# One token-mixing and SwiGLU layer in fp32r: the address of the split weights, 64 bytes further on in two stages

## The chip, the cores and the metric

One core of a Trainium2 chip runs the whole layer in one program. The metric is the device time of an execution in microseconds; lower is better. It is given as the median of several runs.

## The reference

The layer takes x (512 tokens of 2048 channels) and a condition c. It computes six rows of modulation from c, and then

```python
h = x * (1.0 + sc_m) + sh_m
y = mixer_sublayer(h, ...)       # projections, HGRN2, sparse attention, merge, w_out
x = layer_norm(ALPHA * x + (1.0 + gt_m) * y, ln1_g, ln1_b)
h = x * (1.0 + sc_f) + sh_f
y = (silu(h @ w_gate) * (h @ w_up)) @ w_down      # 2048 -> 5632 -> 2048
x = layer_norm(ALPHA * x + (1.0 + gt_f) * y, ln2_g, ln2_b)
```

All of it is float32.

## The kernel before

**Products in three parts.** A float32 operand is split into a rounded high part (type fp32r, made by a copy on ScalarE) and a low part (the difference, made on VectorE). `mm3` (line 239) then issues three matmuls for each product: high by high, high by low, low by high. So every weight block of 128x1024 is loaded from memory into a tile `raw`, ScalarE makes `whi` from it (lines 276 and 351), VectorE makes `wlo` (lines 277 and 363), and TensorE reads both. The names `whi` and `wlo` stand for four tiles each, which are used in turn (NW = 4).

**The stages, in order of time.** First the projections of the mixer, with the scans and the attention between them, then the branches `pa` and `pb`, the output projection w_out, gate/up, and w_down. Every matmul of the projections and of w_out streams 512 columns. In w_out (lines 1320 to 1357) the merged activations `mhi`, `mlo` are loaded into the array and the weights are streamed; the last of its four column blocks, c == 3, goes row block by row block (t = 0 to 3), while LayerNorm (`finish1`, line 1145) starts on the rows that are ready.

**Gate/up and w_down by seven products.** Both are block products in which seven products of quarter size stand for eight (`SEVEN`, line 127). For gate/up there are 44 groups of 128 output columns (22 of gate, 22 of up), and seven steps in each. One step (`gu_product`, line 1383) runs over 8 slices; in each, a 128x128 piece of `whi` or `wlo` is loaded into the array and 256 columns of the activations are streamed past it, three matmuls per slice. The activations lie in `mhi`, `mlo`, or in their block sums `R4` to `R7`. The sums of the weight blocks are made on VectorE (`add_behind`, line 1284) or by adding transfers. `prepare` (line 1299) splits a step's weights three steps ahead. In w_down (`dn_product`, line 1502) it is the other way round: pieces of the factors `fhi`, `flo` (the activations) are loaded into the array, and 512 columns of the weights are streamed. The weights of the last eight steps are kept, two in small tiles (`wkhi`, `wklo`) and six in large ones (`wkeep`), and used at the end (line 1683).

**Where the tiles lie.** Tiles come from pools that are laid out one after the other in a partition of SBUF. From the left: `const`; then the pool named `weights`, which holds five `raw` tiles and the eight tiles of `whi` and `wlo`; then `big`, eight tiles of 8 KB (`hThi`, `hTlo`, `mhi`, `mlo`, `wkeep` and others). From the right: the pool of small tiles (`heap`, later `stay`), then `pass` with the sums `R`, which is released when gate/up's last step has been issued, and in its place the pool `tail` (line 1675), which holds w_down's factors. The lines that the change touches:

```python
wp = ctx.enter_context(tc.tile_pool(name="weights", bufs=NW))
bp = ctx.enter_context(tc.tile_pool(name="big", bufs=8))
...
def pair(self):
    return (wp.tile([P, 1024], FR, name="whi", tag="whi"), wp.tile([P, 1024], FR, name="wlo", tag="wlo"))
```

The pools from the left end at byte 149472, where those from the right begin: the partition is full.

**The order of the work** is written out by hand (`manual_schedule`): each engine gets its instructions in the order in which the code calls them, and waits on semaphores for what they need.

Of the kernel before, what the change touches and what calls it, by code (L numbers as in the profile page):

```python
# [25 lines left out]
FT = mybir.dt.float32  # L26
FR = mybir.dt.float32r
# [4 lines left out]
P = 128  # L32
D = 2048
T = 512
NT = T // P
KD = D // P
# [21 lines left out]
NRAW = 5  # L58
NW = 4
# [81 lines left out]
def layer_kernel(ctx, tc, ws, wa, wada, xt, x, cin, bada, lbl, ghg, gcq, gckv, ln1c, lnrow, ident, lvm, dist, out):  # L141
    nc = tc.nc
    mmul = nc.tensor.matmul

    cp = ctx.enter_context(tc.tile_pool(name="const", bufs=1))
    wp = ctx.enter_context(tc.tile_pool(name="weights", bufs=NW))
    bp = ctx.enter_context(tc.tile_pool(name="big", bufs=8))
    hp = tc.alloc_tile_pool(name="heap", bufs=NHEAP, side="right")
    pp = ctx.enter_context(tc.tile_pool(name="psum", bufs=8, space=bass.MemoryType.PSUM))
    dp = ctx.enter_context(tc.tile_pool(name="dram", bufs=1, space=bass.MemoryType.DRAM))  # L150
# [16 lines left out]
    one_t = cp.tile([P, P], FT, name="one_t")  # L167
    lvm_t = cp.tile([P, 7, 256], U8, name="lvm_t")
    idm_t = cp.tile([P, T], U8, name="idm_t")
    bada_t = cp.tile([P, 96], FT, name="bada_t")  # L170
    ada = cp.tile([P, 96], FT, name="ada")
    ada1 = cp.tile([P, 96], FT, name="ada1")
    lb_t = cp.tile([P, DEPTH, HGH], FT, name="lb_t")
# [3 lines left out]
    ln1c_t = cp.tile([P, 2, KD], FT, name="ln1c_t")  # L177
# [6 lines left out]

    cond = cp.tile([P, D], FT, name="cond", tag="row")
    nc.sync.dma_start(cond[:1], cin)
    nc.scalar.dma_start(bada_t, bada)
    nc.gpsimd.memset(one_t, 1.0)
    nc.gpsimd.memset(eps6, 1e-6)
    nc.gpsimd.memset(eps5, 1e-5)  # L190
# [39 lines left out]
    side = Side()  # L230
# [13 lines left out]

    def ada_dot(raw, j, n, parts):

        init = bada_t[:, j:j + 1] if n == 0 else ada[:, j:j + 1]
        w = D // parts
        nc.vector.tensor_tensor_reduce(raw, raw, cond[:, n * w:n * w + w], scale=1.0, scalar=init,
                                       op0=OP.mult, op1=OP.add, accum_out=ada[:, j:j + 1])  # L250

    keys = first_keys()
# [26 lines left out]
    class Stream:  # L279
# [86 lines left out]
                self.load_to(0)  # L366

        def pair(self):
            return (wp.tile([P, 1024], FR, name="whi", tag="whi"), wp.tile([P, 1024], FR, name="wlo", tag="wlo"))

        def get(self, *key, ahead=2):

# [73 lines left out]
    for k in range(KD):  # L446
# [14 lines left out]
        whi, wlo = W.ready.pop(("A", k))  # L461
# [20 lines left out]
        if k in (1, 2):  # L482

            for t in (2 * k - 2, 2 * k - 1):
                ps = bank("early")
                for kk in range(2):
                    hi, lo = hh(kk)
                    s, w = slice(t * P, t * P + P), slice(kk * T, kk * T + T)
# [182 lines left out]
    t = heap("ki")  # L671
# [3 lines left out]
    for p in range(4):  # L675
        whi, wlo = W.get("iq", p)
        for n in range(2):
            ps = bank("qidx")
            for k in range(4):
                w = slice(n * T + k * P, n * T + k * P + P)  # L680
# [179 lines left out]
    for t in range(NT):  # L860
        s = slice(t * P, t * P + P)
        for n in range(2):
            ps = bank("uv")
            w = slice(n * T, n * T + T)
# [3 lines left out]
            ps = ps.rearrange("p (h v) -> p h v", v=SAV)  # L868
# [193 lines left out]
    for n, blk in enumerate((2, 5)):  # L1062
        cols = slice(blk * 16, blk * 16 + 16)
        nc.vector.tensor_scalar_add(ada1[:, cols], ada[:, cols], 1.0)
        ps = bank("grow")
# [8 lines left out]
        return r  # L1074

    gtm = gate_row(0, "gtm")
    colA = cp.tile([P, KD], FT, name="colA")
    colB = cp.tile([P, KD], FT, name="colB")
    nc.vector.tensor_scalar_add(ada1[:, 64:80], ada[:, 64:80], 1.0)
    nc.vector.tensor_mul(colA, ln1c_t[:, 0], ada1[:, 64:80])  # L1080
    nc.vector.tensor_mul(colB, ln1c_t[:, 1], ada1[:, 64:80])
    nc.vector.tensor_add(colB, colB, ada[:, 48:64])


# [148 lines left out]
    def out_mm(ps, t, i, w, first, last):  # L1233
        for kk in range(2):
            hi, lo = mh(2 * i + kk)
            s = slice(t * P, t * P + P)
            mm3(ps, hi[:, s], lo[:, s], *piece(w, kk), first and kk == 0, last and kk == 1)
# [82 lines left out]
    for c in range(4):  # L1320
        if c < 3:
            xs = passing("x")
            for t in range(NT):
                xin_load(xs[:, t], t, c)
            banks = [bank(f"y{t}") for t in range(NT)]
            for i in range(8):
                w = W.get("out", c, i)
                more(1)
                for t in range(NT):
                    out_mm(banks[t], t, i, w, i == 0, i == 7)  # L1330
        else:
            wl = {i: W.get("out", c, i, ahead=min(2, 7 - i)) for i in range(4)}
        for t in range(NT):
            if c == 3:
                ps = bank("y3")
                z = zt[t] = passing("z")
                for n in range(3):
                    nc.gpsimd.dma_start(z[:, n], d_z[t, n])
                z = z[:, 3]
                xin_load(z, t, c)  # L1340
                order = [4, 5, 6, 7, 0, 1, 2, 3] if t == NT - 1 else range(8)
                if t == NT - 1:
                    fetch_behind(-1)
                for n, i in enumerate(order):
                    if i not in wl:
                        wl[i] = W.get("out", c, i, ahead=min(2, 7 - i))
                    out_mm(ps, t, i, wl[i], n == 0, n == 7)
                    if t == NT - 1 and n in (3, 4, 5):
                        del wl[n + 1]
                        prepare(n - 3)  # L1350
            else:
                ps, z = banks[t], xs[:, t]
            nc.vector.scalar_tensor_tensor(z, z, ALPHA, ps, op0=OP.mult, op1=OP.add)
            nc.vector.bn_stats(st1[t][:, c * 6:c * 6 + 6], z)
            nc.gpsimd.dma_start(d_z[t, c], z)
            if c == 3:
                side.add(t, finish1(t))
    side.add(NT - 1, block_sums())
    del banks, xs, wl, w, ps, z, gtm
    W.scale.clear()  # L1360

    def factor(i, k):
# [279 lines left out]
    for step in range(len(steps)):  # L1642
        u = steps[step]
        if step + 3 < len(steps):
            prepare(step + 3)
        fetch_behind(step)
        for ahead, do in ((4, factor_tiles), (8, factor_load)):
            if step + ahead < len(steps):
                v = steps[step + ahead]
                if v.group[0] == "dn" and v.group[2] == 0:  # L1650
                    do(v.i, v.group[1])
        last = step >= len(steps) - KEEP
        if u.group[0] == "gu":
            gu_product(u)
            gu_use(u)
        elif not last:
            dn_product(u)
            dn_use(u)
        add_behind(step)
        if not last:  # L1660
            u.pair = None
        if step == 4 * NPRE + 2:
            for t in range(NT):
                side.drain(t)
            assert not hraw
        if u.group[0] == "gu" and u.group[1] >= NPRE and u.i in ("q7", "q5"):

            nc.gpsimd.tensor_copy(pace, acc_copy[0])
            more(1)
        if step == nsteps - 1:  # L1670
            del m_hi, m_lo
            mh = None
            sums.clear()
            xp.release()
            yp = ctx.enter_context(tc.tile_pool(name="tail", bufs=24, side="right", reuse_waits="tile"))
            small = lambda name, dt=FT: yp.tile([P, T], dt, name=name, tag="y")
            for i in "EYVR":
                part[i] = big(i, FT)
            side.add(0, base_side())
            side.add(1, end_side())  # L1680
# [3 lines left out]
    for t in range(2):  # L1684
# [14 lines left out]
        z = ys[0]  # L1699
# [117 lines left out]
```

## Time and profile before

| | |
|---|---|
| median of 3 runs | 2781.99 us (2778.76 to 2782.38) |
| the profiled execution | 2779.29 us, its span 2777.5 us |
| mean granted TensorE clock | 0.998 |
| TensorE busy | 2749.9 us, 99% of the span |
| VectorE, ScalarE, GpSimd busy | 74%, 42%, 24% |
| chain that ended last | TensorE 92% |
| w_out, c = 0 to 2 | 1277.43 us on, 130.57 us |
| gate/up | from 1456.74 us to about 2347 us |
| w_down | from there to 2765.7 us |

The profile names an instruction by its line, engine and operation, with the tiles that it writes and reads. PE is TensorE's matmul, PEld its weight load, DVE VectorE, ACT ScalarE. A matmul's duration runs from its start until its last result is out, and the next starts long before that; how fast the engine goes is read from the distance of the starts, or from a stretch of time in which it is busy throughout, divided by the number of matmuls in it.

### The profile page before, as it was taken

How to read it: one execution, taken by the hardware profiler on the slowest of the kernel's cores; microseconds unless marked ns; L12 is line 12 of the kernel's file. 1: busy time of each engine (PE TensorE's matmuls, PEld its weight loads, DVE VectorE, ACT ScalarE, POOL GpSimd, SP SyncE). 2: the span in 40 equal slices, each digit the busy share in tenths (PEclk: the TensorE clock that was granted, in tenths of full speed). 3: DMA queues.
4: the chain of work that ended last, by engine and by line, in shares of the span. 5: the costliest groups of instructions: out<-in, count | busy, mean ns of one | idle time of the engine just before them, and what ended most of it. 6: DMA issues, size and time to landing. Idle time of an engine off the chain costs nothing.

```text
span 2777.5 us, 41873 instructions
## 1 busy us (share of the span) xinstructions
PE 2749.9 (99%) x16090; PEld 2439.6 (88%) x16090; DVE 2050.1 (74%) x2904; ACT 1163.5 (42%) x1736; POOL 670.8 (24%) x911
## 2 busy tenths in 40 slices
PE   8999999999999999999999999999999999999998
PEld 6888888888888888788889999999999999888886
DVE  7887787778862688545668877777777777885688
ACT  4334434332222556222246444444444444554453
POOL 0011133333010575421210212221221222750000
PEclk9999999999999999999999999999999999999999
DMA  9867555555984896997945546666555768987775
GB/s 380 302 232 219 158 165 168 179 180 187 319 288 145 229 284 209 271 285 198 293 152 185 191 167 186 185 172 189 171 196 160 192 175 228 323 304 239 244 251 184
DMA packets 179275, 609.87 MB, mean 220 GB/s; under 512 B 23201, under 2 KB 23505, under 8 KB 176001
## 3 DMA queue, kind: packets, MB, share of 16 engines
q1 hardware_dynamic: 126866, 430.18, 45.2%
q0 software_dynamic: 51776, 176.44, 23.8%
q8 instruction: 126, 2.06, 0.3%
q14 instruction: 75, 0.61, 0.1%
q10 hardware_dynamic: 432, 0.57, 0.1%
HBM read 564.09 MB, written 149.70 MB: 257 GB/s over the span
## 4 chain that ended last, share of the span: by engine, by line
PE 92%; DVE 2%; issue 2%; DMA 2%; POOL 1%; ACT 0%; SPq 0%; POOLq 0%; DVEq 0%; ACTq 0%
PE gb L233 6%; PE ga L233 6%; PE V L241 6%; PE V L242 6%; PE V L243 6%; PE y L233 5%; PE pb L233 3%; PE Y L243 3%; PE Y L242 3%; PE Y L241 3%; PE g L233 3%; PE dnV L242 3%; PE dnV L243 3%; PE dnV L241 3%; PE v L233 3%; PE early L233 3%
## 5 line engine op out<-in xcount | busy, mean ns | idle before, releaser
L277 DVE TENSOR_TENSOR wlo<-raw,whi 128x1024 fp32r<-128x1024 f32 x374 | 472.0, 1269 | 253.7 <-ACT whi L276 251.8
L276 ACT ACTIVATE whi<-raw 128x1024 fp32r<-128x1024 f32 x374 | 395.5, 1058 | 315.9 <-PE dnV L243 106.6
L363 DVE TENSOR_TENSOR wlo<-raw,whi 128x1024 fp32r<-128x1024 f32 (+1 forms) x228 | 284.7, 1252 | 107.7 <-ACT whi L351 107.1
L351 ACT ACTIVATE whi<-raw 128x1024 fp32r<-128x1024 f32 (+1 forms) x228 | 234.0, 1039 | 196.9 <-DVE raw L1090 80.2
L242 PE MATMUL V<-mlo,whi 128*128 128x256 f32 x1024 | 290.1, 283 | 0.0
L243 PE MATMUL V<-mhi,wlo 128*128 128x256 f32 x1024 | 290.1, 283 | 0.0
L241 PE MATMUL V<-mhi,whi 128*128 128x256 f32 x1024 | 290.1, 283 | 0.0
L243 PE MATMUL Y<-R,wlo 128*128 128x256 f32 x704 | 199.4, 283 | 0.0
L242 PE MATMUL Y<-R,whi 128*128 128x256 f32 x704 | 199.4, 283 | 0.0
L241 PE MATMUL Y<-R,whi 128*128 128x256 f32 x704 | 199.4, 283 | 0.0
L241 PEld LDWEIGHTS V<-mhi,whi 128*128 128x128 f32 x1024 | 193.2, 189 | 0.0
L242 PEld LDWEIGHTS V<-mlo,whi 128*128 128x128 f32 x1024 | 193.2, 189 | 0.0
L243 PEld LDWEIGHTS V<-mhi,wlo 128*128 128x128 f32 x1024 | 193.2, 189 | 0.0
L241 PE MATMUL dnV<-whi,fhi 128*128 128x512 f32 x352 | 137.0, 389 | 0.0
L243 PE MATMUL dnV<-whi,flo 128*128 128x512 f32 x352 | 137.0, 389 | 0.0
L242 PE MATMUL dnV<-wlo,fhi 128*128 128x512 f32 x352 | 137.0, 389 | 0.0
L241 PEld LDWEIGHTS Y<-R,whi 128*128 128x128 f32 x704 | 132.8, 189 | 0.0
L243 PEld LDWEIGHTS Y<-R,wlo 128*128 128x128 f32 x704 | 132.8, 189 | 0.0
L242 PEld LDWEIGHTS Y<-R,whi 128*128 128x128 f32 x704 | 132.8, 189 | 0.0
L276 ACT ACTIVATE whi<-wrow 128x1024 fp32r<-128x1024 f32 x80 | 84.4, 1055 | 75.8 <-DVE wrow L1288 75.8
L1001 POOL DMA_DIRECT2D sum_dn<-in_ws x132 | 97.6, 829 | 58.2 <-DMA sum_dn<-in_ws 49.9
L233 PE MATMUL ga<-hThi,whi 128*128 128x512 f32 x256 | 101.8, 398 | 0.0
(473 smaller groups left out, 7786.3 us busy)
## 6 DMA issues: line engine op xcount, KB each, us to landing
raw<-in_ws SPq DMA_DIRECT2D x414, 512.0 KB, 5.2
sum_dn<-in_ws POOLq DMA_DIRECT2D x132, 512.0 KB, 8.6
raw<-in_wada SPq DMA_DIRECT2D x128, 512.0 KB, 5.0
raw<-sum_dn SPq DMA_DIRECT2D x88, 512.0 KB, 4.0
rawb<-in_wada SPq DMA_DIRECT2D x22, 1024.0 KB, 11.9
sum_dn<-sum_dn POOLq DMA_DIRECT2D x44, 512.0 KB, 5.1
wrow<-in_ws SPq DMA_DIRECT2D x40, 512.0 KB, 6.6
sum_gu<-in_ws POOLq DMA_DIRECT2D x24, 512.0 KB, 9.2
```

The costliest lines, as they stand in the source:

```text
L233: mmul(*a, **k)
L241: f(ps, ahi, bhi, start=first, stop=False, **k)
L242: f(ps, ahi, blo, start=False, stop=False, **k)
L243: f(ps, alo, bhi, start=False, stop=last, **k)
L276: nc.scalar.activation(hi, src, AF.Copy)
L277: engine.tensor_sub(lo, src, hi.bitcast(FT))
L351: nc.scalar.activation(hi, src, AF.Copy)
L363: nc.vector.tensor_sub(lo, src, hi.bitcast(FT))
L1001: nc.gpsimd.dma_start(d_sum[g, dst], block(g, src), **({"accum_op": OP.add} if add else {}))
```

## The change

The pool `weights` is split. The five `raw` tiles keep a pool of their own (`raw`) ahead of `big`; `whi` and `wlo` get a pool behind `big`. In the last row block of w_out, when the last streamed weights have been used (n == 3), this pool is released, a pool `shift` of one tile of 16 floats is put in its place, and a pool `weights2` of the same eight tiles behind that: from there on, in gate/up and w_down, `whi` and `wlo` lie 64 bytes further on. When `pass` is released, a pool `shift2` of 64 bytes comes ahead of `tail` from the right, so that w_down's factors lie 64 bytes lower. Room for it comes from three small tiles: the bias of the modulation is loaded straight into the accumulator `ada`, and `colA` and `colB` are made in the place of `ln1c_t`.

The addresses that the built programs give, as the remainder by 128 of the tile's first byte in a partition (all pieces that a matmul reads start a multiple of 512 bytes further on):

| matmuls (fp32r) | streamed operand | loaded operand |
|---|---|---|
| all 5888 with 512, 384, 256 or 128 columns up to and with w_out, before and after | 96 | 96 |
| the 96 of the index scores, before and after | 96 | 96 |
| 7392 of gate/up, 256 columns, before | 96 | 96 |
| 7392 of gate/up, after | 96 | 32 |
| 1848 of w_down, 512 columns, before | 96 | 96 |
| 1728 of w_down, after | 32 | 32 |
| 72 of w_down with `wkeep`, after | 96 | 32 |
| 48 of w_down with factors that are made in the pool `stay`, after | 32 | 96 |

The constant `id_t` (streamed in transposes) and `one_t` have 0 in both.

Every engine has the same instructions in the same order in both programs. What differs beside the addresses is which earlier instruction some of them wait for: the first splits of gate/up's weights wait for a later matmul of w_out than before, since the new tiles overlap two old ones each, and two neighbouring loads of the stored rows (`base`, line 1546) have exchanged a wait.

```diff
--- before.py
+++ after.py
@@ -143,8 +143,9 @@
     mmul = nc.tensor.matmul
 
     cp = ctx.enter_context(tc.tile_pool(name="const", bufs=1))
-    wp = ctx.enter_context(tc.tile_pool(name="weights", bufs=NW))
+    wp = ctx.enter_context(tc.tile_pool(name="raw", bufs=NRAW))
     bp = ctx.enter_context(tc.tile_pool(name="big", bufs=8))
+    wq = [tc.alloc_tile_pool(name="weights", bufs=NW)]
     hp = tc.alloc_tile_pool(name="heap", bufs=NHEAP, side="right")
     pp = ctx.enter_context(tc.tile_pool(name="psum", bufs=8, space=bass.MemoryType.PSUM))
     dp = ctx.enter_context(tc.tile_pool(name="dram", bufs=1, space=bass.MemoryType.DRAM))
@@ -167,7 +168,6 @@
     one_t = cp.tile([P, P], FT, name="one_t")
     lvm_t = cp.tile([P, 7, 256], U8, name="lvm_t")
     idm_t = cp.tile([P, T], U8, name="idm_t")
-    bada_t = cp.tile([P, 96], FT, name="bada_t")
     ada = cp.tile([P, 96], FT, name="ada")
     ada1 = cp.tile([P, 96], FT, name="ada1")
     lb_t = cp.tile([P, DEPTH, HGH], FT, name="lb_t")
@@ -184,7 +184,7 @@
 
     cond = cp.tile([P, D], FT, name="cond", tag="row")
     nc.sync.dma_start(cond[:1], cin)
-    nc.scalar.dma_start(bada_t, bada)
+    nc.scalar.dma_start(ada, bada)
     nc.gpsimd.memset(one_t, 1.0)
     nc.gpsimd.memset(eps6, 1e-6)
     nc.gpsimd.memset(eps5, 1e-5)
@@ -244,9 +244,8 @@
 
     def ada_dot(raw, j, n, parts):
 
-        init = bada_t[:, j:j + 1] if n == 0 else ada[:, j:j + 1]
         w = D // parts
-        nc.vector.tensor_tensor_reduce(raw, raw, cond[:, n * w:n * w + w], scale=1.0, scalar=init,
+        nc.vector.tensor_tensor_reduce(raw, raw, cond[:, n * w:n * w + w], scale=1.0, scalar=ada[:, j:j + 1],
                                        op0=OP.mult, op1=OP.add, accum_out=ada[:, j:j + 1])
 
     keys = first_keys()
@@ -366,7 +365,7 @@
                 self.load_to(0)
 
         def pair(self):
-            return (wp.tile([P, 1024], FR, name="whi", tag="whi"), wp.tile([P, 1024], FR, name="wlo", tag="wlo"))
+            return tuple(wq[0].tile([P, 1024], FR, name=n, tag=n) for n in ("whi", "wlo"))
 
         def get(self, *key, ahead=2):
 
@@ -1074,11 +1073,10 @@
         return r
 
     gtm = gate_row(0, "gtm")
-    colA = cp.tile([P, KD], FT, name="colA")
-    colB = cp.tile([P, KD], FT, name="colB")
+    colA, colB = ln1c_t[:, 0], ln1c_t[:, 1]
     nc.vector.tensor_scalar_add(ada1[:, 64:80], ada[:, 64:80], 1.0)
-    nc.vector.tensor_mul(colA, ln1c_t[:, 0], ada1[:, 64:80])
-    nc.vector.tensor_mul(colB, ln1c_t[:, 1], ada1[:, 64:80])
+    nc.vector.tensor_mul(colA, colA, ada1[:, 64:80])
+    nc.vector.tensor_mul(colB, colB, ada1[:, 64:80])
     nc.vector.tensor_add(colB, colB, ada[:, 48:64])
 
 
@@ -1345,8 +1343,16 @@
                     if i not in wl:
                         wl[i] = W.get("out", c, i, ahead=min(2, 7 - i))
                     out_mm(ps, t, i, wl[i], n == 0, n == 7)
+                    if t == NT - 1 and n == 3:
+                        for k in range(4, 8):
+                            del wl[k]
+
+                        del w
+                        wq[0].release()
+                        shift = ctx.enter_context(tc.tile_pool(name="shift", bufs=1))
+                        shift.tile([P, 16], FT, name="shift")
+                        wq[0] = ctx.enter_context(tc.tile_pool(name="weights2", bufs=NW, reuse_waits="tile"))
                     if t == NT - 1 and n in (3, 4, 5):
-                        del wl[n + 1]
                         prepare(n - 3)
             else:
                 ps, z = banks[t], xs[:, t]
@@ -1356,7 +1362,7 @@
             if c == 3:
                 side.add(t, finish1(t))
     side.add(NT - 1, block_sums())
-    del banks, xs, wl, w, ps, z, gtm
+    del banks, xs, wl, ps, z, gtm
     W.scale.clear()
 
     def factor(i, k):
@@ -1672,6 +1678,9 @@
             mh = None
             sums.clear()
             xp.release()
+
+            shift2 = ctx.enter_context(tc.tile_pool(name="shift2", bufs=1, side="right"))
+            shift2.tile([P, 16], FT, name="shift2")
             yp = ctx.enter_context(tc.tile_pool(name="tail", bufs=24, side="right", reuse_waits="tile"))
             small = lambda name, dt=FT: yp.tile([P, T], dt, name=name, tag="y")
             for i in "EYVR":
```

## Rows read from the trace of the kernel before

**Rows 1.** The page, part 1: busy us (share of the span) xinstructions.

```profile
PE 2749.9 (99%) x16090; PEld 2439.6 (88%) x16090; DVE 2050.1 (74%) x2904; ACT 1163.5 (42%) x1736; POOL 670.8 (24%) x911
```

**Rows 2.** Stretches: us, busy by engine (xinstructions), clock, DMA share, GB/s; gate/up, w_down.

```profile
core 0: us, PE busy (x) PEld busy (x) DVE busy (x) ACT busy (x) POOL busy (x), PEclk, DMA share, GB/s
1540.30:2346.90 806.60, 806.60 (x6724) 806.60 (x6723) 621.94 (x703) 368.98 (x503) 168.40 (x300) 1.00 0.62 181
2346.90:2765.70 418.80, 418.80 (x1850) 346.84 (x1849) 328.35 (x351) 207.63 (x251) 102.08 (x81) 1.00 0.78 265
```

**Rows 3.** The chain that ended last, in w_out: start us, us, what.

```profile
1277.43 130.57 PE y L233 x576
```

**Rows 4.** Lines by form, TensorE: count | busy us, mean ns of one.

```profile
L241 PE MATMUL V<-mhi,whi 128*128 128x256 f32 x1024 | 290.1, 283 | 0.0
...
L241 PE MATMUL dnV<-whi,fhi 128*128 128x512 f32 x352 | 137.0, 389 | 0.0
...
L241 PEld LDWEIGHTS V<-mhi,whi 128*128 128x128 f32 x1024 | 193.2, 189 | 0.0
```

**Rows 5.** Timeline in gate/up, matmuls and loads: start us, us, engine, line, operation.

```profile
1599.92 0.28 PE L243 MATMUL V<-mhi,wlo 128*128 128x256 f32 x1
1600.04 0.29 PE L241 MATMUL V<-mhi,whi 128*128 128x256 f32 x1
...
1599.93 0.19 PEld L241 LDWEIGHTS V<-mhi,whi 128*128 128x128 f32 x1
1600.05 0.19 PEld L242 LDWEIGHTS V<-mlo,whi 128*128 128x128 f32 x1
```

**Rows 6.** Lines 198 and 1166: timeline, then durations min/median/max of matmul and load.

```profile
14.79 1.39 PE L198 MATMUL cond<-one_t 128*128 128x128 f32 x11
L198 PE MATMUL cond<-one_t x29: 275/275/276, 14.8 to 17.9; 128*128 128x128 f32 x29
L198 PEld LDWEIGHTS cond<-one_t x56: 192/192/334, 9.5 to 18.0; 128*128 128x128 f32 x56
1435.94 1.03 PE L1166 MATMUL zt<-id_t,z 128*128 128x128 f32 x8
...
L1166 PE MATMUL zt<-id_t,z x64: 270/272/328, 1423.2 to 1467.1; 128*128 128x128 f32 x64
L1166 PEld LDWEIGHTS zt<-id_t,z x64: 138/140/143, 1423.0 to 1467.0; 128*128 128x128 f32 x64
```

**Rows 7.** Timeline of score matmuls with 512 columns.

```profile
930.13 0.40 PE L233 MATMUL s<-rlo,qb 128*128 128x512 f32 x1
930.36 0.62 PE L233 MATMUL s<-rhi,qb 128*128 128x512 f32 x2
930.82 0.39 PE L233 MATMUL s<-rlo,qb 128*128 128x512 f32 x1
931.05 0.39 PE L233 MATMUL s<-rhi,qb 128*128 128x512 f32 x1
931.28 0.39 PE L233 MATMUL qb<-rhi,whi 128*128 128x512 f32 x1
```

**Rows 8.** Timelines where w_out ends and gate/up begins.

```profile
1450.18 0.39 PE L233 MATMUL y<-whi,mlo 128*128 128x512 f32 x1
...
1452.00 2.04 ACT L276 ACTIVATE whi<-raw 128x1024 fp32r<-128x1024 f32 x2
...
1453.25 2.35 DVE L277 TENSOR_TENSOR wlo<-raw,whi 128x1024 fp32r<-128x1024 f32 x2
...
1456.74 0.28 PE L241 MATMUL V<-mhi,whi 128*128 128x256 f32 x1
```

**Rows 9.** Gate/up on VectorE: its longest wait (us, times, longest), then lines by form.

```profile
DVE wlo L277 <- ACT whi L276: 157.8, 129, 1.6
L277 DVE TENSOR_TENSOR wlo<-raw,whi 128x1024 fp32r<-128x1024 f32 x202 | 245.4, 1223 | 159.4 <-ACT whi L276 157.8
...
L1297 DVE TENSOR_TENSOR raw<-raw,wrow 128x1024 f32<-128x1024 f32 x40 | 48.7, 1218 | 0.0
```

## The prediction

> **What bounds the kernel now.** I read the busy shares first [rows 1]. TensorE is busy for 2749.9 of 2777.5 us and no other engine is over 75%, so only a change in what TensorE itself does, or a wait put in front of it, can move the end. The profiled execution took 2779.29 us around that span, 2.7 us below the median of 2781.99 us; I make the sum in differences and put it on the median.
>
> Then the table of stretches [rows 2]. [...] With 6724 matmuls there, one starts every 806.60 / 6724 = 120.0 ns (the few records that the edges cut shift this by less than 0.1 ns). The w_down stretch gives 418.80 / 1850 = 226.4 ns, and the first three column blocks of w_out 130.57 / 576 = 226.7 ns [rows 3]. The reader should note in the lines by form that the durations of single matmuls (283 and 389 ns) and loads (189 ns) are latencies that overlap [rows 4]; the pace is what sums to the span.
>
> The pace splits in two. [...] So 256 columns are worth 106.7 ns, and 13.3 ns remain on every matmul, at 256 and at 512 columns alike. In gate/up there are 44 groups of 7 products, each of 8 slices of three matmuls, 7392 in all: the remainder is 7392 x 13.3 ns = 98.6 us there. Next to each matmul a weight load for the next one begins some 10 ns after the matmul does [rows 5], so a load and a streamed operand are under way at the same time. By place I mean what is left of a tile's byte address when it is divided by 128. Before the change both operands of every one of these matmuls have the place 96. The change makes that 32 against 96 for gate/up, and for nothing else that is large.
>
> **The change, part by part.**
>
> *Order of the work.* No engine gets an instruction more or less or in another order. So every cost must come from an address, or from a wait that an address moves.
>
> *Gate/up's weights 64 bytes further on: 7392 matmuls with 256 columns.* The trace has no such matmul with operands at two places, so I bound it. Gain, largest: the whole remainder goes, 98.6 us. Gain, by a row: the transposes (line 1166) are the only matmuls in quantity whose operands have different places, 0 and 96; eight of them take (1.03 - 0.27) / 7 = 108.6 ns apiece [rows 6]; at that pace gate/up would lose 7392 x 11.4 = 84 us. They are another operation, with a shorter load (140 ns against 189), so this is an end and no forecast. Between: the full fp32 matmuls of line 198 have both operands at place 0, a similar load (the median is 192 ns), and take (1.39 - 0.275) / 10 = 111.5 ns [rows 6]. So a load of this size does not in itself force 120 ns; at 111.5 the gain would be 62.8 us. Loss: the nearest row is the score matmuls of qb at 512 columns, which go at 1.15 / 5 = 230 ns from 930.13 to 931.28 us [rows 7], 3.3 ns over the 226.7 of the same form elsewhere; 7392 x 3.3 = +24 us. Nothing excludes a loss altogether.
>
> I take half of the remainder: 120.0 to 113.3 ns, 7392 x 6.67 ns = **49 us** less. My reason: a load reads 512 bytes of a partition while the matmul reads 1024, so the faster stream overruns a lead of 64 bytes soon, and I expect the two to be kept apart in only part of each load. 113.3 is close to the 111.5 of line 198, the row with the nearest load, and on the careful side of it.
>
> [...]
>
> *w_down's factors 64 bytes down.* There the weights stream and the factors are loaded. Both move by 64 bytes modulo 128, so 1728 of 1848 matmuls keep equal places (32 and 32). The other 120 get places 64 bytes apart: 72 with the kept weights of the last steps, 48 with the factors made before the new pool exists. Even the whole remainder on them is 120 x 13.3 = 1.6 us either way. I put 0.
>
> *The new pool's waits.* Its first tiles lie over two old ones each, so the splits of the first three gate/up weights must now wait for the last matmul that reads the old weights. That one starts at 1450.18 us; ScalarE makes the first whi at 1452.00 and VectorE the first wlo at 1453.25 [rows 8]. What holds them is ScalarE's work on the transposes before, and the raw weights are there. Cost 0; if that cover were gone, the slack to the first gate/up matmul at 1456.74 would still be over 2 us.
>
> *Smaller edits.* The bias of the adaLN rows is read into the accumulator, and the two LayerNorm columns are scaled in place: same instructions, same sizes, 0. In the tail pool two neighbouring loads of stored rows exchange a wait and are issued in the same order, 0.
>
> *What is late next.* With 113.3 ns the gate/up stretch of 806.6 us shrinks to 761.6. VectorE's 621.94 us [rows 2] go from 77% to 82% of it, ScalarE's from 46% to 48%. VectorE's longest waits there are for ScalarE's whi, 157.8 us in 129 pieces, none over 1.6 us [rows 9]; they are the room in that chain, and by the code weights are split three steps (3 x 24 x 113.3 ns = 8.2 us) ahead. DMA has a share of 0.62. I put 0 for a new bound.
>
> Sum: 2781.99 - 49 = **2733 us** (2730 against the profiled execution's own 2779.29).
>
> **Rivals.** *No effect.* The remainder is a fixed cost of changing weights and has nothing to do with places. For it: it is the same 13.3 ns at 256 and 512 columns, in every stage, whichever buffer the tiles lie in, as a fixed cost would be; a clash of two streams should feel their length. [...] Against it: line 198 changes weights as often and shows 111.5 [rows 6]. Time: 2782, give or take 5.6 us, the 0.2% that a measurement of this kernel can tell from no change.
>
> *Slower.* The equal place is the good one. If the offset makes the streamed operand overtake the load, the load may be held up instead of the matmul, and with 256 columns it has no spare time: one begins with each matmul, and the next 120 ns on. With 512 columns it has twice that, which is why such a clash could hide in the rest of the kernel. It decides once the pace passes 120.8 ns (0.75 ns x 7392 = 5.6 us). Priced by the 3.3 ns of the qb rows: 2782 + 24 = 2806. For it: a load shows 189 ns beside a pace of 120 [rows 4], so it is the longer of the two. Against it: line 198 shows loads going in every 111.5 ns.
>
> *Part of the gain is lost.* TensorE would go at 113.3, but the splits come late at the denser places of each group of seven steps, where four block sums of 1.22 us and seven splits of 1.22 us [rows 9] stand on VectorE. If a third is given back: 2782 - 33 = 2749. For it: VectorE is at 77% already. Against it: the waits there are VectorE's, not TensorE's.
>
> **Numbers.** Forecast 0.50, part lost 0.12, no effect 0.20, slower 0.18; so faster 0.62, same 0.20, slower 0.18. The range runs from 2698, the 84 us of the transposes' pace, up to 2790, which takes in no effect and the mildest losses; most of the slower case is left out above, and the loss of the whole remainder below.
>
> **What would show it.** The gate/up stretch at 1.00 clock should hold 6724 matmuls in about 762 us, while the w_out stretch keeps 226.7 ns and w_down about 226.4. If gate/up stays at 120.0, the fixed cost was right. If it is over 120.8 and the loads show more than 189 ns, the slower rival. If single starts are 113 apart but gaps with VectorE as releaser stand between the steps, part was lost. A change of w_down's pace, or of any stage before 1456 us, would mean that something other than the relative place matters, and my reading is wrong at its root.

## The result, and the profile after

The changed kernel takes 2747.48 us (median of 20 executions), the kernel before 2780.6 us beside it. The ratio is that of the means, 2758.63 and 2780.72 us: 0.9921, 95% interval 0.9895 to 0.9946. It is faster, by 22 us where 49 were forecast. The median hides the shape: 12 of the 20 executions lie between 2744 and 2749 us and 8 between 2772 and 2781, none between. I call these the lower and the upper group; the median falls in the lower one, and so is 33 us under the one before. The profiled execution (2745.55 us, span 2743.8, mean granted clock 0.998) is of the lower one.

The page of the changed kernel, part 1, answers to [rows 1]:

```profile
PE 2716.5 (99%) x16090; PEld 2391.9 (87%) x16090; DVE 2044.0 (74%) x2904; ACT 1158.0 (42%) x1736; POOL 688.3 (25%) x911
```

As many instructions as before, on every engine, and TensorE still fills the span. So the time went in TensorE's pace. Stretches of the changed kernel, with the columns of [rows 2]; the first two lie in gate/up, the third in w_down:

```profile
core 0: us, PE busy (x) PEld busy (x) DVE busy (x) ACT busy (x) POOL busy (x), PEclk, DMA share, GB/s
1580.00:1980.00 400.00, 400.00 (x3532) 400.00 (x3531) 326.52 (x369) 189.41 (x263) 100.12 (x160) 1.00 0.63 191
2000.00:2280.00 280.00, 280.00 (x2473) 280.00 (x2473) 228.21 (x260) 132.42 (x185) 73.68 (x115) 1.00 0.65 191
...
2400.00:2700.00 300.00, 300.00 (x1287) 241.38 (x1286) 218.92 (x245) 146.82 (x172) 27.49 (x21) 1.00 0.76 250
```

Gate/up: 400.00 / 3532 = 113.25 ns, and 113.3 from start to start (the matmuls cut by the edges make such quotients 0.1 to 0.3 ns too small). That is the forecast to the digit. But w_down goes at 300.00 / 1287 = 233.1 ns, 233.3 from start to start, where it went at 226.7. That was not forecast. The lines by form say the same in latencies, against 283 and 389 ns in [rows 4]:

```profile
L241 PE MATMUL V<-mhi,whi 128*128 128x256 f32 x1024 | 282.7, 276 | 0.0
...
L241 PE MATMUL dnV<-whi,fhi 128*128 128x512 f32 x352 | 138.9, 395 | 0.0
```

The account by stage, from the starts of the first and the last matmul of each:

| stage | before, us | after, us | difference |
|---|---|---|---|
| up to gate/up | 1456.7 | 1458.0 | +1.2 |
| gate/up | 890.2 | 843.4 | -46.8 |
| w_down | 418.7 | 430.4 | +11.8 |
| the end behind it | 11.8 | 11.8 | 0.0 |
| span | 2777.5 | 2743.8 | -33.7 |

Gate/up starts between 1456.0 and 1459.7 us in the profiles below, with the same work ahead of it, so the first row is scatter. The third is some 1700 matmuls times 6.67 ns (11.4 us), and a little from those that have other addresses.

One more thing stands in the early part of gate/up. This is the timeline of TensorE in the changed kernel around one short stall:

```profile
1497.76 0.28 PE L242 MATMUL Y<-R,whi 128*128 128x256 f32 x1
1497.87 0.28 PE L243 MATMUL Y<-R,wlo 128*128 128x256 f32 x1
1497.99 0.28 PE L241 MATMUL Y<-R,whi 128*128 128x256 f32 x1
1498.11 0.28 PE L242 MATMUL Y<-R,whi 128*128 128x256 f32 x1
1498.82 0.38 PE L243 MATMUL Y<-R,wlo 128*128 128x256 f32 x1 [0.43 <-DVE wlo L276]
...
1500.08 0.28 PE L241 MATMUL Y<-R,whi 128*128 128x256 f32 x1
1500.19 0.28 PE L242 MATMUL Y<-R,whi 128*128 128x256 f32 x1
1500.31 0.28 PE L243 MATMUL Y<-R,wlo 128*128 128x256 f32 x1
1500.42 0.28 PE L241 MATMUL Y<-R,whi 128*128 128x256 f32 x1
```

Ahead of the stall 117.8 ns from start to start, behind it 113.3. The same operands at the same addresses have two paces here, and TensorE changed from one to the other where it had stood still. After the last such stall (1564 us) the remaining 6503 matmuls keep 113.3. What TensorE waited for between 1455 and 2300 us (the waits view; the first row is the transposes, line 1166 in [rows 6], the last of which stand between gate/up's first steps; the row of PEld is the stall at 1564 us, where the matmul itself stood for 0.1 us):

```profile
PE zt L1164 <- DVE z L1153: 1.2, 2, 0.8
PE Y L243 <- DVE wlo L276: 0.4, 1, 0.4
PE A L243 <- DVE wlo L276: 0.2, 1, 0.2
...
PEld V L241 <- ACT e L1418: 0.3, 1, 0.3
```

### The profile page after: what moved, and what is told of

Same layout as the page of the kernel before. It is cut to its first block, busy times and chain, and to the rows that moved or that the text cites. A ratio compares the mean times of both kernels' runs of the same rounds, so it can differ in the third digit from the quotient of the medians.

```text
span 2743.8 us, 41871 instructions
## 1 busy us (share of the span) xinstructions
PE 2716.5 (99%) x16090; PEld 2391.9 (87%) x16090; DVE 2044.0 (74%) x2904; ACT 1158.0 (42%) x1736; POOL 688.3 (25%) x911
## 4 chain that ended last, share of the span: by engine, by line
PE 90%; DVE 3%; DMA 2%; issue 2%; ACT 2%; POOL 1%; SPq 0%; DVEq 0%; ACTq 0%; POOLq 0%
PE gb L233 6%; PE y L233 6%; PE ga L233 6%; PE V L241 5%; PE V L243 5%; PE V L242 5%; PE early L233 3%; PE g L233 3%; PE dnV L241 3%; PE dnV L243 3%; PE dnV L242 3%; PE v L233 3%; PE pb L233 3%; PE Y L243 3%; PE Y L241 3%; PE Y L242 3%
## 5 line engine op out<-in xcount | busy, mean ns | idle before, releaser
L243 PE MATMUL V<-mhi,wlo 128*128 128x256 f32 x1024 | 282.8, 276 | 0.0
L241 PE MATMUL V<-mhi,whi 128*128 128x256 f32 x1024 | 282.7, 276 | 0.0
L242 PE MATMUL V<-mlo,whi 128*128 128x256 f32 x1024 | 282.7, 276 | 0.0
L241 PE MATMUL Y<-R,whi 128*128 128x256 f32 x704 | 194.4, 276 | 0.0
L242 PE MATMUL Y<-R,whi 128*128 128x256 f32 x704 | 194.4, 276 | 0.0
L248 DVE CUSTOM_DVE_ANT_0 raw<-raw,cond,ada 128x1024 f32<-128x1024 f32 x128 | 166.5, 1314 | 1.1 <-DMA raw<-in_wada 0.8
```

The source lines that it names most:

```text
L241: f(ps, ahi, bhi, start=first, stop=False, **k)
L242: f(ps, ahi, blo, start=False, stop=False, **k)
L243: f(ps, alo, bhi, start=False, stop=last, **k)
```

## The experiments

Two theories stand against my prediction's account. **By 256:** what counts is the difference D between the byte address of the loaded operand and that of the streamed one, modulo 256. Before the change D is 0 in gate/up and w_down. After it gate/up has D = 64, and w_down 128 (factors at 160, weights at 32), which modulo 128 looks like 0. **Two paces:** where a D has two paces, the start after a stall settles which, and the two groups of times are executions that end up in the one or the other. The rival to the first is that w_down suffers from something else in the new pools; to the second, that the upper group is a matter of clock, chip or another stage.

All edits are to the changed kernel. Its two shift tiles have 16 floats (64 bytes) each.

**w_down equal modulo 256.**

```diff
-            shift2.tile([P, 16], FT, name="shift2")
+            shift2.tile([P, 48], FT, name="shift2")
```

> The changed kernel with 192 bytes instead of 64 ahead of w_down's factors, so that streamed weights and loaded factors have the same address modulo 256 (32 and 32) and not only modulo 128 (32 and 160 in the changed kernel). Theory A, what counts is the difference of the two addresses modulo 256: w_down goes back from 233.3 to 226.7 ns a matmul, gate/up stays at 113.3; 1728 x 6.67 ns = 11.5 us less than the changed kernel, 2734 us against its 2745.5. Theory B, what counts is each operand's address modulo 128 (both 32 in either kernel): w_down stays at 233.3 ns, 2745 us. Theory C, w_down's slowing has nothing to do with addresses but follows from gate/up ending sooner: also 233.3 ns.

Median 2733.72 us of 6 (5 between 2732.0 and 2736.1, one at 2764.3), ratio 0.9853, interval 0.9822 to 0.9884. Its stretches in gate/up and w_down:

```profile
1580.00:1980.00 400.00, 400.00 (x3532) 400.00 (x3531) 325.76 (x368) 189.28 (x262) 100.09 (x160) 1.00 0.63 191
...
2400.00:2700.00 300.00, 300.00 (x1326) 248.39 (x1325) 227.73 (x259) 154.27 (x186) 27.94 (x21) 1.00 0.78 258
```

w_down is back at 226.7 ns (300.00 / 1326 = 226.2), gate/up keeps 113.3, and the lower group lies 11 us under that of the changed kernel, which is what w_down's term comes to. The 64 bytes by which the diff moved the factors cost these 11 us; moved by 192 they cost 0.6 (w_down takes 419.3 us here and 418.7 before). Theories B and C, with 233.3 ns, fall. Weights 64 bytes up and factors 192 down are 256 apart in sum, so at 512 columns a period of 256 is shown (226.7 ns at 0 and at 256) and not a longer one; at 256 columns the runs go from 0 to 192 and don't test it. The time is the forecast's number, by a kernel that isn't the one forecast.

**The changed kernel beside itself.**

> The changed kernel itself once more, for its two groups of times (2744 to 2749 us and 2772 to 2781 us). If the groups belong to the chip or to one loading of the program, all runs here fall in one of them; if each execution falls anew, both appear, about one in three in the upper. If its profile is of the upper group: gate/up at 120.0 ns with w_down at 226.7 would mean that both changed paces are gone together (2780); gate/up at 120.0 with w_down at 233.3 would give 2792, above what was seen; gate/up at 113.3 with long waits would mean something off TensorE.

Eleven executions on one chip: 5 between 2744.1 and 2745.4, 6 between 2771.9 and 2775.6. Both groups occur on one chip, from one execution to the next.

**D = 128 and D = 192 in gate/up.**

```diff
-                        shift.tile([P, 16], FT, name="shift")
+                        shift.tile([P, 32], FT, name="shift")
```

with `shift2` as in the changed kernel, so that w_down gets D = 64:

> Gate/up's weights 128 bytes further on instead of 64 (difference 128 modulo 256, equal modulo 128), w_down's factors as in the changed kernel, which gives w_down a difference of 64 modulo 256. Theory A: gate/up at a pace of its own, neither 120.0 nor 113.3 necessarily, and slower than 120.0 if 256 columns behave as 512 did at a difference of 128 (126.7 ns, +49 us); w_down near the 229 to 230 ns that the 120 odd matmuls of the changed kernel showed. Theory B (modulo 128): gate/up at 120.0, as before the change, w_down at about 229.

2781.56 us. And the same line with 48 floats, which gives gate/up D = 192 and w_down D = 0 with both operands at 160:

> Gate/up's weights 192 bytes further on (difference 192 modulo 256; 64 modulo 128, as in the changed kernel), w_down's factors as in the changed kernel, so that w_down has equal addresses modulo 256, both 160. Theory A: w_down at 226.7 ns although both operands moved; gate/up not necessarily at 113.3, since 192 is not 64. Theory B: gate/up at 113.3, and w_down at 233.3, since both operands have 32 modulo 128 as in the changed kernel.

2765.02 us. Gate/up and w_down, first for D = 128 and 64:

```profile
1580.00:1980.00 400.00, 400.00 (x3373) 400.00 (x3373) 311.40 (x351) 182.66 (x251) 85.26 (x150) 1.00 0.62 182
...
2400.00:2700.00 300.00, 300.00 (x1288) 241.70 (x1287) 222.64 (x234) 146.87 (x172) 55.95 (x40) 1.00 0.76 252
```

then for D = 192 and 0:

```profile
1580.00:1980.00 400.00, 400.00 (x3399) 400.00 (x3398) 313.47 (x355) 184.91 (x254) 86.77 (x150) 1.00 0.62 182
...
2400.00:2700.00 300.00, 300.00 (x1325) 248.40 (x1324) 227.76 (x242) 150.80 (x177) 53.69 (x38) 1.00 0.79 258
```

From start to start: 118.7 and 233.3 ns, then 117.8 and 226.7. Equal places are good for the 512 columns of w_down (226.7) wherever both lie (0 by difference: at 224, 32 or 160), and bad for the 256 columns of gate/up (120.0). With D = 192 TensorE never stands still after 1469 us, so that run can't tell a single pace of 117.8 from the upper of two. Theory B falls in both runs: it had 120.0 and 229, then 113.3 and 233.3. Theory A held in the pace of its own at 128 and in w_down's 226.7, but its bracket for w_down at D = 64, 229 to 230, was 3 to 4 ns low.

**Stops in gate/up and w_down.** The four runs that follow make TensorE stand still 26 times, at every 16th step, 17 times in gate/up and 9 in w_down:

```diff
+    for n in range(40, len(steps) - 16, 16):
+        steps[n].stop = True
+
+    def stop(ps, e):
+
+        nc.vector.scalar_tensor_tensor(e, ps[:, :1], 0.0, e.bitcast(FT), op0=OP.mult, op1=OP.add)
...
+            if k == 3 and u.stop:
+                stop(ps, wlo[:, 4 * P:4 * P + 1])
```

(and a like call in w_down's loop). The next matmul needs that column of wlo, VectorE needs the sum as it stands. First with D = 64 and 0, as in the first experiment:

> The kernel with both pools moved (gate/up 64 bytes apart, w_down equal modulo 256) and 26 stops: at every 16th step VectorE reads one column of the running sum and rewrites one column of the second half of wlo with its own value (0 times the sum added), so that TensorE stands still once for some 0.5 to 3 us and starts anew. Theory (which of two locked paces TensorE falls into is settled when it starts after standing still): every one of the 17 stretches of gate/up between stops holds one pace from its first ten matmuls on, 113.3 or 117.8 ns, both appear, and changes happen at stops alone; w_down stays at 226.7 in all its stretches. Rival (113.3 is the pace of this address and 117.8 is a matter of the early part of gate/up, its other instructions or the DMA traffic there): 113.3 in all 17 stretches. Rival (the pace drifts with load or time): changes between stops. The time is some 2734 plus 26 stops of 0.5 to 3 us, 2750 to 2810.

The stops were longer than expected, since VectorE's own work stands ahead of them (in the 6.00 us from 1969 us on, within one stop, VectorE is busy for 4.37): 2.1 to 6.5 us from start to start in gate/up, and behind 15 of the 17 there the granted clock was 0.50 for some 3 to 6 us. So the time, 2882.70 us, is over the range I gave, and says nothing here. The paces do. A stop in the timeline of TensorE:

```profile
1968.79 0.28 PE L243 MATMUL V<-mhi,wlo 128*128 128x256 f32 x1
1974.69 0.58 PE L241 MATMUL V<-mhi,whi 128*128 128x256 f32 x1 [5.63 <-DVE wlo L1395]
1975.07 0.41 PE L242 MATMUL V<-mlo,whi 128*128 128x256 f32 x1
```

and stretches between four successive stops, at a granted clock of 1.00:

```profile
1940.00:1968.00 28.00, 28.00 (x250) 28.00 (x248) 22.39 (x25) 12.25 (x17) 3.17 (x7) 1.00 0.57 194
1985.00:2020.00 35.00, 35.00 (x299) 35.00 (x298) 25.88 (x31) 16.64 (x22) 2.92 (x7) 1.00 0.47 159
2030.00:2065.00 35.00, 35.00 (x312) 35.00 (x311) 28.36 (x32) 16.54 (x23) 7.02 (x14) 1.00 0.49 156
```

112.0, 117.1 and 112.2 ns by the quotients; from start to start 113.3, 117.8 and 113.3. Of the 17 stretches behind stops 14 have 113.3 and 3 have 117.8, each the same to its end once the first ten matmuls at a clock of 1.00 are past (from there on its sixths agree to a few hundredths of a nanosecond), none in between. The clock (1.00 in all three rows), the share of DMA (0.47 at 117.8 ns, 0.49 and 0.57 at 113.3) and the instructions don't go with it. The nine stretches of w_down, at D = 0, all have 226.7.

The same with D = 192 in gate/up:

> The same 26 stops, with the gate/up weights 192 bytes further on instead of 64 (w_down equal modulo 256 again). In the run without stops gate/up stayed at 117.8 ns from first to last and TensorE never stood still. Theory (192 is 64 seen from the other operand and has the same two paces; that run merely started in the slower one and had no stall to leave it): some of the 17 stretches at 113.3. Rival (192 has the one pace 117.8): 117.8 in all 17. Time 2765 plus the stops, 2780 to 2840.

2888.97 us, over the range for the same reason. Three successive stretches of gate/up:

```profile
1640.00:1675.00 35.00, 35.00 (x299) 35.00 (x298) 25.94 (x28) 16.33 (x23) 2.91 (x7) 1.00 0.52 169
1685.00:1720.00 35.00, 35.00 (x312) 35.00 (x310) 27.57 (x33) 16.87 (x23) 7.63 (x13) 1.00 0.56 160
1740.00:1772.00 32.00, 32.00 (x274) 32.00 (x274) 22.43 (x27) 13.90 (x20) 7.44 (x13) 1.00 0.64 160
```

D = 192 has the same two paces, with the other one as the usual one: 2 of 17 at 113.3, 15 at 117.8. The rival of a pace of its own falls.

Then D = 96 in both stages, and D = 32 in both (weights 24 and 8 floats on, factors 16 and 48 down):

> The same 26 stops, gate/up 96 bytes apart modulo 256 and w_down 96 bytes apart too (weights 96 bytes on, tail pool 64 down). Theory (the pace goes by the difference modulo 256, in steps as fine as 32 bytes): gate/up between the paces of 64 and 128, 113.3 to 118.7, and w_down 233.3, the pace of its neighbours 64 and 128. Rival (only the difference in units of 64 bytes counts): 96 gives just the paces of 64, or just those of 128.

> The same 26 stops, gate/up 32 bytes apart modulo 256 and w_down 32 too (weights 32 bytes on, tail pool 192 down). Theory (fine steps): gate/up between the paces of 0 and 64, 113.3 to 120.0, w_down 226.7 to 233.3. Rival (units of 64 bytes): gate/up as at 0, 120.0 in all stretches, and w_down 226.7 in all.

2893.10 and 2896.66 us. Stretches of gate/up and one of w_down, for D = 96 and then for 32:

```profile
1640.00:1675.00 35.00, 35.00 (x297) 35.00 (x296) 26.20 (x31) 16.14 (x22) 3.47 (x8) 1.00 0.47 155
1835.00:1870.00 35.00, 35.00 (x301) 35.00 (x300) 28.71 (x33) 15.80 (x24) 8.48 (x13) 1.00 0.68 182
2435.00:2465.00 30.00, 30.00 (x130) 24.12 (x129) 23.07 (x20) 14.69 (x17) 17.75 (x11) 1.00 0.80 277
...
1690.00:1725.00 35.00, 35.00 (x298) 35.00 (x298) 28.04 (x33) 15.96 (x22) 8.86 (x15) 1.00 0.50 144
2435.00:2470.00 35.00, 35.00 (x152) 28.18 (x151) 26.07 (x24) 16.82 (x19) 20.02 (x16) 1.00 0.85 307
```

From start to start, with 96 gate/up has 117.3 in 6 stretches and 118.7 in 11, w_down 234.3 in all nine; with 32 it is 118.3 in all 17 and 233.3. So 32 bytes matter, and the rival that counts in units of 64 falls. My bracket for 96, between 113.3 and 118.7, held; for w_down I was 1 ns low.

**The upper group.** Twice the changed kernel once more, for a profile of an execution in the upper group:

> The changed kernel once more, to see an execution of the upper of its two groups of times (2772 to 2781 against 2744 to 2749 us). Theory: where the time is in the upper group, gate/up's pace after its last stall (some 1564 us) is 117.8 ns to the end, 4.4 ns x 6503 matmuls = 29 us more, and w_down the same 233.3; where it is in the lower group, 113.3. Rival: the upper group has 113.3 too, and its 27 us are elsewhere (a lower clock, stalls, another stage).

> As the run before it: 117.8 ns in gate/up after the last stall if its time is over 2770 us, 113.3 if it is under 2750.

2744.94 and 2744.74 us: both lower, with 113.3 as in the first profile, so they tell nothing of the upper one.

**The weights' pool alone.**

```diff
-            shift2 = ctx.enter_context(tc.tile_pool(name="shift2", bufs=1, side="right"))
-            shift2.tile([P, 16], FT, name="shift2")
```

> Only the weights' new pool, 64 bytes further on; w_down's factors stay where they were before the change. Then w_down's difference is 192 modulo 256 (the factors' address less the weights'). Theory (difference modulo 256): w_down at the 229.0 to 229.6 ns that 120 matmuls with this difference showed in other runs, 1752 x 2.7 ns = 4.7 us over the kernel with both at the same place, so a lower group at 2738 to 2739 us, an upper one at some 2768. Rival (equal places modulo 128 are good for w_down, 64 apart is bad, as my prediction had it): w_down at up to 233.3 ns, 11.7 us over, 2745 to 2746.

Four executions between 2734.8 and 2737.6 us, one at 2777.8. The changed kernel on the same chip took 2744.9 and 2744.7 us, so half of the change alone is 8.5 us better than the whole, in the lower group: the second half, the factors' move, did only harm. The profile is of the one at 2777.8, with a granted clock of 0.997 like the others:

```profile
1580.00:1980.00 400.00, 400.00 (x3399) 400.00 (x3398) 313.65 (x354) 183.17 (x251) 86.75 (x150) 1.00 0.63 183
...
2400.00:2700.00 300.00, 300.00 (x1288) 242.99 (x1287) 221.34 (x233) 145.49 (x170) 52.56 (x39) 1.00 0.76 251
```

Gate/up is at 117.8 from 1470 us to its end, without a stall, and w_down at 233.3, where I had expected 229.0 to 229.6 for D = 192. The lower group lies under the 2738 to 2739 that I had expected, the upper one over its 2768. No profile of this kernel shows the lower group. But in every kernel with gate/up at D = 64 the first 48 matmuls of w_down have D = 192 (the factors made in the pool `stay`). The second and the 47th of them are shown here, first of the first experiment's profile, then of a profile of the same kernel in the upper group (2764.44 us, see below):

```profile
2303.39 0.39 PE L242 MATMUL dnV<-wlo,fhi 128*128 128x512 f32 x1
2313.69 0.39 PE L242 MATMUL dnV<-wlo,fhi 128*128 128x512 f32 x1
...
2331.58 0.40 PE L242 MATMUL dnV<-wlo,fhi 128*128 128x512 f32 x1
2342.08 0.40 PE L242 MATMUL dnV<-wlo,fhi 128*128 128x512 f32 x1
```

10.30 / 45 = 228.9 ns and 10.50 / 45 = 233.3. So D = 192 has two paces at 512 columns too. With both, 7331 x 4.4 = 32 us in gate/up and 1752 x 4.4 = 8 us in w_down are the distance between this kernel's groups, 41.6 us (an estimate for the lower group, from the 228.9 of the other kernel).

**One stall less.** On the kernel with w_down equal modulo 256, three sums of the first group of seven steps come one step earlier:

```diff
-            adds.setdefault(s - ahead, []).append((("gu", n), what))
+            early = n == NPRE and what in ("S3", "S1", "S2")
+            adds.setdefault(s - ahead - early, []).append((("gu", n), what))
```

> The kernel with w_down equal modulo 256, and for the first group of seven steps three weight sums on VectorE one step earlier, so that the stall at 1563 to 1566 us (0.34 and 0.22 us) goes. Theory (the pace is drawn at each start after a stall, and the last one decides): no stall after 1501 us, the pace holds from there to the end; the lower group at 2733 to 2734 us, and executions in the upper group (2764) are left only where the start at 1500 us falls badly, fewer than the 6 to 7 in 10 lower ones that two draws in a row would give. Rival (what decides is something else, such as the chip or the moment): the same share of upper executions as without the edit, or the stall moves to another place.

Median 2733.38 us, five executions between 2731.8 and 2735.2, ratio 0.9833, interval 0.9819 to 0.9846. The stall at 1563 us is gone. Whether that keeps executions out of the upper group, five can't say, so it ran again beside the kernel without the edit, and the changed kernel with them:

> The kernel with w_down equal modulo 256 again, beside the next one on the same chip: lower group 2732 to 2736, upper some 2764 (1 of 6 so far). If two draws in a row decide, at 19 good in 24 each as the stopped run showed, some 4 in 10 executions are in the upper group; if it is rarer, the draws at these starts are better than those after long stops.

> The three sums early again: median 2733.4 as before, and if the last stall was worth a draw, fewer upper executions than the run beside it; if the share is the same in both, the stall at 1563 us has nothing to do with it.

> The changed kernel again, with more executions, for the share of the upper group (so far 13 of 33) and for a profile of one. Theory: a profile at 2772 us or more shows gate/up at 117.8 ns from its last stall to its end and w_down at 233.3; one under 2750 shows 113.3. Rival: 113.3 in both, the difference elsewhere.

Without the edit 2733.95 us (one of 6 in the upper group, at 2764.4), with it 2734.20 (2 of 6, at 2763.6 and 2764.7), the changed kernel 2759.55 (6 of 12; median between the groups). With the earlier runs it is 2 of 12 and 2 of 11: the edit did nothing that can be seen, and the idea that this stall was a draw worth saving isn't borne out. Nor are the 4 in 10 that two draws at 19 in 24 would give; the stretches counted above make the chance of one draw 14 in 17.

But two of these profiles fell in the upper group. The kernel without the edit, at 2764.44 us, around 1497 us:

```profile
1496.38 0.28 PE L241 MATMUL Y<-R,whi 128*128 128x256 f32 x1
1496.49 0.28 PE L242 MATMUL Y<-R,whi 128*128 128x256 f32 x1
1497.61 0.39 PE L243 MATMUL Y<-R,wlo 128*128 128x256 f32 x1 [0.84 <-DVE wlo L276]
...
1499.48 0.28 PE L243 MATMUL Y<-R,wlo 128*128 128x256 f32 x1
1499.60 0.28 PE L241 MATMUL Y<-R,whi 128*128 128x256 f32 x1
```

and its stretches:

```profile
1500.00:2300.00 800.00, 800.00 (x6794) 800.00 (x6794) 630.06 (x720) 371.12 (x514) 172.42 (x298) 1.00 0.62 184
...
2400.00:2700.00 300.00, 300.00 (x1325) 248.41 (x1324) 229.08 (x243) 151.81 (x177) 51.70 (x38) 1.00 0.79 260
```

113.3 ahead of the stall, 117.8 behind it and for all 7077 matmuls that remain (800.00 / 6794 = 117.75), with w_down at 226.7 and the clock at 1.00. 7077 x 4.4 ns = 31 us is the distance from 2733.7 to 2764.4. The second profile, at 2763.62 us, shows the same. The upper group is the upper pace; a lower clock or another stage has no part in it. At 117.8 the splits keep up and TensorE doesn't stand still any more (busy for all 800.00 us), not even at 1563 us, so that the upper pace, once it has come through 1500 us, stays to the end. That the changed kernel's own upper group is the same is argued from its distance (some 31 us): its five profiles were all of the lower group.

The paces from start to start that the profiles of these runs show, in nanoseconds:

| D, bytes | 256 columns (gate/up) | 512 columns (w_down) |
|---|---|---|
| 0 | 120.0 | 226.7 |
| 32 | 118.3 | 233.3 |
| 64 | 113.3 or 117.8 | 233.3 |
| 96 | 117.3 or 118.7 | 234.3 |
| 128 | 118.7 (120.0 in the first 48) | 233.3 |
| 192 | 113.3 or 117.8 | 228.9 or 233.3 |

The 72 matmuls with `wkeep`, also at D = 192 in the changed kernel, go at 229.5 within their short runs. Of the 1728 in the prediction's count 24 read kept weights that lie in the factors' own pool and have D = 0 in every kernel.

## Why the prediction was wrong, step by step

**Gate/up's pace** was right: 113.3 ns, and 46.8 of the 49 us in the profiled execution. The rest went to four stalls of 0.2 to 0.7 us and to the early part at 117.8. With not an instruction more or less, the pace went from 120.0 to 113.3 ns by where the loaded and the streamed operand lie; that it is their reads that clash fits this, but no run shows the mechanism. That the number came out to the digit is luck: it was half of a remainder. That remainder of 13.3 ns is my estimate too, 120.0 less the 106.7 by which 226.7 is above it; no run shows it as a part of a matmul, and what the runs show in its place is 113.3 to 120.0 ns at 256 columns, by D. And the reason that I gave for half of the remainder, a lead of 64 bytes that is soon overrun, isn't shown by anything. By it a lead of 128 should have done better, and it measured 118.7.

**w_down's factors: this step failed.** I wrote "Both move by 64 bytes modulo 128, so 1728 of 1848 matmuls keep equal places" and put 0. Both moved, but in opposite directions, +64 and -64, and what counts in the runs at 512 columns is the difference modulo 256, which became 128 (233.3 ns, where 0 has 226.7). The term measured +11.8 us, and the first experiment takes all but 0.6 of it away by an edit of one number. Nothing in the trace had told me 128; every matmul of the large stages had D = 0 there, so 128 and 256 fitted equally well, and I should have priced the other one: the 3.3 ns of the qb rows [rows 7] at 512 columns would have been 1728 x 3.3 = 6 us, half of the loss. The prediction named this sign itself: a change of w_down's pace would show its reading wrong at its root.

**Two paces at one address** weren't among the rivals, and so were put at nothing. Before the change D = 0 had shown only one (120.0 ns in gate/up), and the sum takes a single pace for all executions. 8 of 20 lie 31 us higher, which is 12.5 us in the mean. So of the 27 us between the forecast of 49 and the 22 of the means, 2.5 went in gate/up itself, 11.8 in w_down and some 12.5 to the upper pace.

*No effect* and *slower* fell with the pace. *Part of the gain is lost* gave 2749, close to the median by chance: TensorE's waits for VectorE's splits in gate/up are 0.6 us in the waits view, not 16, and what was lost was lost in w_down and by the second pace. **The new pool's waits** at 0 and **the smaller edits** at 0 held, and no new bound came: VectorE is at 82% in gate/up (326.52 of 400.00 us), as forecast. The median lies in the range of 2698 to 2790.

## What to carry to other kernels

Where a matmul and the weight load for the next one run side by side, as in these fp32r products, try the difference of their two addresses modulo 256 as you would try a tile size. Here it was worth 5.6% of the pace with 256 columns, and 3% the other way with 512, so give each stage its own and move one pool at a time. Compare paces from start to start, not busy shares, which stayed at 99% here. And time such a kernel often enough to see whether its executions fall into groups; a median between two groups is no time that any execution took.

The best version here is the kernel with w_down equal modulo 256 (2733.72 and 2733.95 us in two sets), 0.985 of the time before.

## What the runs showed of the hardware that was not expected

- The same matmul and load at the same addresses ran at 113.3 or at 117.8 ns for thousands of instructions; which it was changed only where TensorE had stood still, if only for some 0.04 us (with the three sums early, one start comes 153 ns after the other at 1480.5 us, 113.3 ahead of it and 117.8 behind). With D = 64 the lower one came behind 14 of 17 stops, with 192 behind 2 of 17. What in the start settles it stays open: long and short stops, with a clock of 0.50 behind them and without, were followed by both.
- Gate/up began at 117.8 in all 13 profiles with D = 64 or 192, right behind w_out's end, and left it only at a stall.
- The pace was carried on from one stage to the next: with gate/up at D = 64, w_down's first matmuls, at D = 192, went at 228.9 ns in the profiles where gate/up ended at 113.3, and at 233.3 in the three where it ended at 117.8. Why 64 bytes help 256 columns (120.0 to 113.3 ns) and hurt 512 (226.7 to 233.3) stays open.
- The upper group holds 20 of 45 executions of the changed kernel (one expectation above says 13 of 33 where 14 is right), but 4 of 23 of the two kernels with w_down equal, which don't differ from it until gate/up ends. Whether that is chance wasn't tried further.
